# Three direct tiles instead of four, sixteen low halves of weights by adding transfers, and a written order of ScalarE and VectorE while x first arrives

## The chip, the cores and the metric

The kernel runs on one core of a Trainium2 chip. The time is that of the device in microseconds (us); before the change it is 864.02 us, the median of three runs (863.29 to 864.94). Lower is better. The engines are TensorE (PE, with its weight loads PEld), VectorE (DVE), ScalarE (ACT), GpSimd (POOL) and SyncE (SP); transfers are issued by SP, ACT or POOL and carried by 16 DMA engines.

## The reference

One decoder layer on x of 512 tokens by 1024 features, float32. A SwiGLU block, a mixing block and a second SwiGLU block each add to x:

```python
x = x + 0.5 * swiglu(rms_norm(x, g_ffn1[l]), w_ffn1_gate[l], w_ffn1_up[l], w_ffn1_down[l])
h = rms_norm(x, g_mix[l])
# attention, convolution and memory heads of h @ w_in
x = x + jnp.concatenate([y_attn, y_conv, y_mem], axis=-1) @ w_out[l]
x = x + 0.5 * swiglu(rms_norm(x, g_ffn2[l]), w_ffn2_gate[l], w_ffn2_up[l], w_ffn2_down[l])

def swiglu(x, w_gate, w_up, w_down):
    return (jax.nn.silu(x @ w_gate) * (x @ w_up)) @ w_down
```

The inner width of a SwiGLU block is 2816, which is 22 tiles of 128.

## The kernel before

x lies as eight tiles (k = 0 to 7) of 128 features by 512 tokens. A product of float32 operands is made of three matmuls: each operand is a high half (a copy rounded to the matmul's type) and a low half (the operand minus its high half), and `mm3` (L350 to L352) multiplies high by low, low by high and high by high. So each weight tile is split too. `Weights` does that for every load in a fixed list: SP's queue loads a raw tile of 128x1024, ScalarE copies the high half (L170), VectorE subtracts it from the raw tile (L171). Four raw buffers and four buffers of split weights turn by; a load is issued three items ahead of the split, and a split is written three items ahead of its use.

A SwiGLU block has 22 tiles f. The first `N_DIRECT` tiles are *direct*: 24 matmuls 128x512 for gate and 24 for up. Each later tile is *fast*: seven products of half width by a scheme like Strassen's (L447 to L449), 84 matmuls 128x256, on sums of weights (`make_sums`) and on sums of blocks of x (`blocks(k)`, k = 0 to 3, whose high and low halves are bh and bl). `evac` and `hidden` turn gate and up into the high and low half of a hidden tile (hh, hl). The product with the down weights comes in `ROUNDS`: as soon as the hidden tiles of a round exist, their part of all eight output tiles is computed and added to x, as items strewn between the fast tiles (`steps`), and the last round behind tile 21. Round 0 uses matmuls of full width, the others two halves. The first four results of round 0 are added to x by DMAs on POOL's queue (L506), others by VectorE (L509).

The norm's factor per token is found beside the first tile: squares of x on ScalarE (L372), sums on VectorE or POOL (L376), four small matmuls with `ones` (L381, `stats`), a chain on VectorE, then four transposes (L394) into `rb` (`spread`). The direct tiles run on x times the gain, and the factor `rb` comes in at `evac`. At the start x arrives in five loads (`STARTS`), and the weights of tile 0, w0 and w1, in two pieces each between them (`PIECES`), which `split_piece` splits (L182). At the end of the first block and of the mixing block, each finished tile of x is scaled and split (L361, L362) and its square added to the sum, for the norm of the next block. Items of the list have numbers: in the second SwiGLU block w130 and w131 are gate and up of tile 0, w132 and w133 of tile 1.

Apart from a few hand-written stretches a scheduler sets the order of each engine's instructions from the order of the code and the dependences; `tc.manual_schedule(engines=...)` keeps the written order for the engines named.

Of the kernel before, what the change touches and what calls it, by code (L numbers as in the profile page):

```python
# [38 lines left out]
P = 128  # L39
# [21 lines left out]
PIECES = {(0,): slice(0, 512), (2, 3): slice(512, 1024)}  # L61
# [15 lines left out]
ROUNDS = [(0, 4), (4, 8), (8, 12), (12, 16), (16, 18), (18, 22)]  # L77
N_DIRECT = 4
# [8 lines left out]
class Weights:  # L87
# [5 lines left out]
    def __init__(self, nc, pool, dma_ahead, conv_ahead, bufs):  # L93
        self.nc, self.pool = nc, pool
        self.dma_ahead, self.conv_ahead, self.bufs = dma_ahead, conv_ahead, bufs
        self.loads, self.items = [], []
        self.raw, self.after, self.split, self.piece = {}, {}, {}, {}
        self.sums = {}
        self.extra = None
        self.by_hand = 2  # L100
        self.loaded = self.done = self.at = self.turn = 0

    def add(self, ap, off=WIDE):
# [28 lines left out]

    def load_to(self, n):
        while self.loaded < min(n, len(self.loads)):
# [4 lines left out]
            if i >= self.by_hand:  # L139
                to = raw[:, : int(np.prod(ap.shape[1:]))]  # L140
                if len(ap.shape) == 3:
                    to = to.rearrange("p (a b) -> p a b", a=ap.shape[1])
                self.nc.sync.dma_start(to, ap)
            self.loaded += 1

    def split_to(self, n):
        nc = self.nc
        while self.done < min(n, len(self.items)):
# [17 lines left out]
            if i < self.by_hand:  # L166
                self.piece[i] = (src(), hi, lo)
            else:
                raw = src()
                nc.scalar.copy(hi[:, :cols], raw[:, :cols])  # L170
                nc.vector.tensor_tensor(lo[:, :cols], raw[:, :cols], hi[:, :cols].bitcast(F32), op=ALU.subtract)  # L171
# [5 lines left out]
    def load_piece(self, i, c):  # L177
        self.nc.sync.dma_start(self.piece[i][0][:, c], self.loads[i][:, c])
# [18 lines left out]
def steps(f):  # L197
# [4 lines left out]
    m = KT // per_load(0)  # L202
    if r == 1:
        i = f - ROUNDS[1][0]
        return [(0, g) for g in range(m - 1)] if i == 0 else [], [(0, m - 1)] if i == 1 else [], []

    queue = [(q, g) for q in range(1, len(ROUNDS) - 1) for g in range(KT // per_load(q))]
    return [], [queue[f - ROUNDS[2][0]]], []


def layer(tc, ctx, a):
# [35 lines left out]
    def ffn_weights(n, memory):  # L247
# [48 lines left out]

    nc.scalar.dma_start(par, a["par"])
    warm = tmp.tile([P, T], BF16, tag="t", name="warm", bufs=5)
# [7 lines left out]
    W.split_to(2)  # L306
    for ks in STARTS:
        nc.sync.dma_start(x[:, ks[0] : ks[-1] + 1], a["xT"][:, ks[0] : ks[-1] + 1])
        if ks in PIECES:
            for i in range(2):  # L310
                W.load_piece(i, PIECES[ks])
    W.load_to(4)
    nc.scalar.dma_start(ident, a["ident"])
# [50 lines left out]
    class Norm:  # L364
# [5 lines left out]
        def add(self, d, engine=POOL):  # L370
            sq = work() if d else tmp.tile([P, T], F32, tag="sqsum", name=nm("sqsum"), bufs=1)
            ACT.activation(sq, x[:, d], AF.Square)  # L372
            if d == 0:
                self.sum = sq
            else:
                (engine if d < KT - 1 else DVE).tensor_tensor(self.sum, self.sum, sq, op=ALU.add)  # L376

# [12 lines left out]
        def spread(self):  # L390
# [4 lines left out]
            DVE.tensor_copy(rb, ps)  # L395

    def ffn(pool, norm, first, gain, hooks, next_gain, last):
# [123 lines left out]
        for f in range(NF):  # L521
# [6 lines left out]
            else:  # L528
                g, u = (sc_bank(), sc_bank()) if f % 3 == 2 else (mm_bank(), mm_bank())
                gh, gl = W.next()  # L530
                if f == 0:
                    uh, ul = W.next()
                    for ks in first:
                        mm3(g, gh, gl, ks, xhk, xlk, ks[0] == 0, ks[-1] == 7)
                        mm3(u, uh, ul, ks, xhk, xlk, ks[0] == 0, ks[-1] == 7)
                    norm.stats()
                    held = (g, u)
                else:
# [29 lines left out]
    for ks in STARTS:  # L568
        for k in ks:
            scaled_split(k, C_G1)  # L570
        if ks in PIECES:
# [666 lines left out]
```

## Time and profile before

| | |
|---|---|
| median of three runs | 864.02 us |
| profiled execution | 864.32 us, of which 861.8 us are the span of the trace |
| matmuls of 128x256, fast tiles (L447 to L449) | 3 x 864, 716.0 us of printed durations |
| matmuls of 128x512, direct tiles (L350 to L352 with xh, xl) | 3 x 192, 226.7 us of printed durations |
| weights' high halves (L170), all forms | 122 and 72, 199.7 us on ACT |
| weights' low halves (L171), all forms | 122 and 72, 232.5 us on DVE |
| read from DRAM | 85.45 MB, 102 GB/s over the span |

A row of the trace's timeline gives start and duration in us, engine, line, operation and the tiles (out<-in) with their shape, then in brackets how long the engine was idle before it and what released it. A row of the waits gives who waited for whom, the us in total, how often, and the longest. Matmuls overlap, so the printed durations of TensorE add up to more than the time that they take.

### The profile page before, as it was taken

To read this page: it belongs to the slowest core of one execution; us is meant where nothing else is said; L and a number is where in the kernel's file an instruction comes from. 1 tells how busy PE (TensorE), PEld (TensorE's weight loads), DVE (VectorE), ACT (ScalarE), POOL (GpSimd) and SP (SyncE) were. 2 spreads that over 40 slices of the span, in tenths; PEclk is the share of its full clock that TensorE was granted. 3 is DMA by queue.
4 is the path that set the end of the run, shared out by engine and by line. 5 is a ranking of instruction groups with operands and counts; after the bars stand their busy time and mean duration, and the time that the engine had idled before them with its cause. 6 is when DMAs were issued, how large, how long until landed. Compare 5 with 4: busy or idle time off the path is not lost.

```text
span 861.8 us, 15658 instructions
## 1 busy us (share of the span) xinstructions
PE 854.5 (99%) x6361; PEld 790.9 (92%) x6361; DVE 696.6 (81%) x1163; ACT 445.9 (52%) x741; POOL 27.4 (3%) x30
## 2 busy tenths in 40 slices
PE   8999999999999999999999999999999999999998
PEld 5889999999999999988776888889999999999998
DVE  7998987777868797869988985998887868687772
ACT  7455555455644454533948763454654545545540
POOL 0010000000000000300000021010000000000000
PEclk9999999999999999999999999999999999999999
DMA  7335334243553334222010322335334343333312
GB/s 274 122 97 152 100 101 129 86 127 119 141 163 104 122 110 129 82 90 62 19 43 14 116 93 93 102 87 159 99 98 124 98 123 95 109 92 115 107 49 99
DMA packets 34808, 91.44 MB, mean 106 GB/s; under 512 B 3248, under 2 KB 5808, under 8 KB 34736
## 3 DMA queue, kind: packets, MB, share of 16 engines
q1 hardware_dynamic: 32000, 85.99, 32.0%
q0 software_dynamic: 1584, 2.88, 2.0%
q10 hardware_dynamic: 1152, 1.57, 0.6%
q8 instruction: 50, 0.82, 0.4%
q14 instruction: 22, 0.18, 0.1%
HBM read 85.45 MB, written 2.10 MB: 102 GB/s over the span
## 4 chain that ended last, share of the span: by engine, by line
PE 97%; DVE 1%; ACT 1%; DMA 1%; issue 0%; SPq 0%; ACTq 0%; DVEq 0%
PE mm L350 16%; PE mm L352 15%; PE mm L351 15%; PE mm L449 11%; PE mm L448 11%; PE mm L447 11%; PE sc L449 2%; PE sc L448 2%; PE sc L447 2%; PE tp L951 1%; PE sc L352 1%; PE sc L350 1%; PE sc L351 1%; PE sc L880 1%; PE tp L965 1%; PE mm L880 1%
## 5 line engine op out<-in xcount | busy, mean ns | idle before, releaser
L447 PE MATMUL mm<-bh,w 128*128 128x256 f32 x864 | 238.8, 276 | 0.0
L448 PE MATMUL mm<-bl,w 128*128 128x256 f32 x864 | 238.6, 276 | 0.0
L449 PE MATMUL mm<-bh,w 128*128 128x256 f32 x864 | 238.6, 276 | 0.0
L351 PE MATMUL mm<-hl,w 128*128 128x256 f32 (+1 forms) x640 | 183.7, 288 | 0.0
L352 PE MATMUL mm<-hh,w 128*128 128x256 f32 (+1 forms) x640 | 183.6, 287 | 0.0
L350 PE MATMUL mm<-hh,w 128*128 128x256 f32 (+1 forms) x640 | 183.1, 287 | 0.0
L170 ACT CAST w<-wraw 128x1024 fp32r<-128x1024 f32 (+2 forms) x122 | 124.0, 1020 | 86.1 <-PE mm L352 25.1
L171 DVE TENSOR_TENSOR w<-wraw,w 128x1024 fp32r<-128x1024 f32 (+2 forms) x122 | 144.5, 1189 | 28.4 <-ACT w L170 23.1
L447 PEld LDWEIGHTS mm<-bh,w 128*128 128x128 f32 x864 | 162.2, 188 | 0.2
L448 PEld LDWEIGHTS mm<-bl,w 128*128 128x128 f32 x864 | 162.2, 188 | 0.1
L449 PEld LDWEIGHTS mm<-bh,w 128*128 128x128 f32 x864 | 162.2, 188 | 0.0
L351 PEld LDWEIGHTS mm<-hl,w 128*128 128x128 f32 x640 | 120.1, 188 | 2.6 <-DVE hl L406 0.2
L352 PEld LDWEIGHTS mm<-hh,w 128*128 128x128 f32 x640 | 120.2, 188 | 2.5
L350 PEld LDWEIGHTS mm<-hh,w 128*128 128x128 f32 x640 | 120.1, 188 | 2.4
L171 DVE TENSOR_TENSOR w<-s,w 128x1024 fp32r<-128x1024 f32 x72 | 88.0, 1223 | 41.5 <-PE mm L449 34.6
L170 ACT CAST w<-s 128x1024 fp32r<-128x1024 f32 x72 | 75.7, 1051 | 24.8 <-PE mm L449 20.4
L350 PE MATMUL mm<-xh,w 128*128 128x512 f32 x192 | 75.8, 399 | 0.6 <-ACT w L182 0.6
L351 PE MATMUL mm<-xl,w 128*128 128x512 f32 x192 | 75.6, 394 | 0.6 <-DVE xl L362 0.5
L352 PE MATMUL mm<-xh,w 128*128 128x512 f32 x192 | 75.3, 392 | 0.0
L509 DVE SCALAR_TENSOR_TENSOR x<-mm,x 128x512 f32<-128x512 f32 x80 | 54.0, 683 | 1.8 <-PE mm L352 1.8
L468 ACT ACTIVATE t<-t 128x512 f32<-128x512 f32 x36 | 22.8, 633 | 61.7 <-DVE t L467 61.7
L127 DVE TENSOR_TENSOR s<-wraw 128x512 f32<-128x512 f32 x36 | 24.9, 691 | 28.8 <-DMA wraw<-in_wgu 28.6
(244 smaller groups left out, 1370.5 us busy)
## 6 DMA issues: line engine op xcount, KB each, us to landing
wraw<-in_wgu SPq DMA_DIRECT2D x86, 512.0 KB, 3.6
wraw<-in_wd SPq DMA_DIRECT2D x44, 512.0 KB, 3.6
wraw<-in_win SPq DMA_DIRECT2D x12, 512.0 KB, 3.5
x<-t POOLq DMA_DIRECT2D x8, 256.0 KB, 4.5
out<-t SPq DMA_DIRECT2D x7, 256.0 KB, 2.0
x<-in_xT SPq DMA_DIRECT2D x3, 512.0 KB, 6.3
wraw<-in_wout_a SPq DMA_DIRECT2D x6, 256.0 KB, 2.6
wraw<-in_wgu SPq DMA_DIRECT2D x4, 256.0 KB, 4.7
```

The source lines that it names most:

```text
L127: nc.vector.tensor_tensor(s12[:, l], u[:, l], u[:, r], op=ALU.add)
L170: nc.scalar.copy(hi[:, :cols], raw[:, :cols])
L171: nc.vector.tensor_tensor(lo[:, :cols], raw[:, :cols], hi[:, :cols].bitcast(F32), op=ALU.subtract)
L350: PE.matmul(ps[:, t], wh[:, w], hi(k)[:, t], start=one, stop=False, skip_group_check=cut > 1)
L351: PE.matmul(ps[:, t], wh[:, w], lo(k)[:, t], start=False, stop=False, skip_group_check=cut > 1)
L352: PE.matmul(ps[:, t], wl[:, w], hi(k)[:, t], start=False, stop=end, skip_group_check=cut > 1)
L447: PE.matmul(ps, wh[:, c], bh[k][:, block], start=one, stop=False, skip_group_check=not first)
L448: PE.matmul(ps, wh[:, c], bl[k][:, block], start=False, stop=False, skip_group_check=not first)
L449: PE.matmul(ps, wl[:, c], bh[k][:, block], start=False, stop=end, skip_group_check=not first)
L468: ACT.activation(g, g, AF.Silu)
L509: DVE.scalar_tensor_tensor(o, ps, 0.5, xd, op0=ALU.mult, op1=ALU.add)
L880: PE.matmul(banks[h][:, i * ML + c.start : i * ML + c.stop], self.q[rows, n * P : (n + 1) * P], self.kt[rows, ks], start=True, stop=True, ...
```

## The change

There are three parts.

1. `N_DIRECT` goes from 4 to 3, so tile 3 of each SwiGLU block becomes a fast tile, and the rounds become (0,3), (3,7), (7,11), (11,15), (15,19), (19,22). All four loads of round 0's down weights (128x768 each) are used ahead of tile 3. `hidden(f)` follows each direct tile, and the last direct tile also makes the blocks of k = 3.
2. Sixteen loads are marked `by_queue`: in each SwiGLU block the four of round 0, and gate and up of tile 2 in the first block and of tiles 0 to 2 in the second. For these ScalarE writes the negated high half into the low half's place, and a DMA on POOL's queue adds the weights onto it from DRAM.
3. At the start the pieces of w0 and w1 are columns 0 to 256, 256 to 512 and 512 to 1024, split behind k = 0, 2 and 4; the first ones come over ScalarE's queue, and `ident` comes on SP's queue. The order of ScalarE and SP while the loads are issued, and of ScalarE and VectorE in splits and squares, is the written one. In tile 0 the matmuls of gate and up alternate for the x tiles that arrive alone or in twos. `rb` is copied by ScalarE.

```diff
-PIECES = {(0,): slice(0, 512), (2, 3): slice(512, 1024)}
+PIECES = {0: slice(0, 256), 2: slice(256, 512), 4: slice(512, 1024)}
-ROUNDS = [(0, 4), (4, 8), (8, 12), (12, 16), (16, 18), (18, 22)]
-N_DIRECT = 4
+ROUNDS = [(0, 3), (3, 7), (7, 11), (11, 15), (15, 19), (19, 22)]
+N_DIRECT = 3
...
                 nc.scalar.copy(hi[:, :cols], raw[:, :cols])
-                nc.vector.tensor_tensor(lo[:, :cols], raw[:, :cols], hi[:, :cols].bitcast(F32), op=ALU.subtract)
+                if i in self.by_queue:
+                    nc.scalar.activation(lo[:, :cols], hi[:, :cols].bitcast(F32), AF.Copy, scale=-1.0)
+                    nc.gpsimd.dma_start(self.shaped(lo, self.loads[need]), self.loads[need], accum_op=ALU.add)
+                else:
+                    nc.vector.tensor_tensor(lo[:, :cols], raw[:, :cols], hi[:, :cols].bitcast(F32), op=ALU.subtract)
...
-    m = KT // per_load(0)
     if r == 1:
-        i = f - ROUNDS[1][0]
-        return [(0, g) for g in range(m - 1)] if i == 0 else [], [(0, m - 1)] if i == 1 else [], []
+        return [(0, g) for g in range(KT // per_load(0))] if f == N_DIRECT else [], [], []
...
-    return [], [queue[f - ROUNDS[2][0]]], []
+    i = f - ROUNDS[2][0]
+    return [], [queue[i]], queue[i + 1 :] if f == NF - 1 else []
...
-                W.add(down(*d), OTHER if d[0] else WIDE)
+                W.add(down(*d), OTHER if d[0] else WIDE, d[0] == 0)
             if f < N_DIRECT:
-                W.add(flat(gu[f, 0]))
-                W.add(flat(gu[f, 1]))
+                for i in range(2):
+                    W.add(flat(gu[f, i]), WIDE, n == 2 or f > 1)
...
+    W.split_to(2)
+    first = tc.manual_schedule(engines={mybir.EngineType.Activation, mybir.EngineType.SP})
+    first.__enter__()
     nc.scalar.dma_start(par, a["par"])
+    for i in range(2):
+        W.load_piece(i, PIECES[0], nc.scalar)
...
-    nc.scalar.dma_start(ident, a["ident"])
+    nc.sync.dma_start(ident, a["ident"])
+    first.__exit__(None, None, None)
...
-            DVE.tensor_copy(rb, ps)
+            ACT.copy(rb, ps)
...
+                        for k in ks:
+                            w = slice(k * P, (k + 1) * P)
+                            for i, (one, two) in enumerate(((0, xh), (0, xl), (1, xh))):
+                                for ps, both in ((g, (gh, gl)), (u, (uh, ul))):
+                                    PE.matmul(ps, both[one][:, w], two[k], start=k == i == 0, stop=k == 7 and i == 2)
...
-                    if f == 1:
-                        hidden(1, raw[1])
+                    hidden(f, raw[f])
                     blocks(f)
                 if f == N_DIRECT - 1:
-                    for i in range(2, N_DIRECT):
-                        hidden(i, raw[i])
+                    blocks(f + 1)
...
+    with tc.manual_schedule(engines={mybir.EngineType.Activation, mybir.EngineType.DVE}):
+        for k in range(KT):
             scaled_split(k, C_G1)
-        if ks in PIECES:
-            for i in range(2):
-                W.split_piece(i, PIECES[ks])
-    W.split_to(3)
-    for k in range(KT):
-        norm.add(k, DVE)
+            if k in PIECES:
+                for i in range(2):
+                    W.split_piece(i, PIECES[k])
+            if k in (3, 5):
+                sqs[k // 4] = norm.square(k // 4)
+            if k == 6:
+                take(0)
+                take(1)
+        W.split_to(3)
+        for k in range(2, KT):
+            sqs[k] = norm.square(k)
+            if k > 2:
+                take(k - 1)
+        take(KT - 1)
```

What the change moves is seen best in the instruction rows (line, operation, out<-in, shape). First ScalarE at the start of the program; xh is the high half of an x tile, a square's output is sqsum or t, and w0 and w1 are gate and up of tile 0. Before:

```order
L361 ACTIVATE xh_3_119<-x_69,par_67 128x512
L372 ACTIVATE sqsum_19_166<-x_69 128x512
L182 CAST w0_93<-wraw0_92 128x512
L182 CAST w1_95<-wraw1_94 128x512
L361 ACTIVATE xh_5_127<-x_69,par_67 128x512
L372 ACTIVATE t_20_168<-x_69 128x512
L361 ACTIVATE xh_7_131<-x_69,par_67 128x512
L372 ACTIVATE t_21_171<-x_69 128x512
L361 ACTIVATE xh_9_135<-x_69,par_67 128x512
L182 CAST w0_93<-wraw0_92 128x512
L182 CAST w1_95<-wraw1_94 128x512
```

and the same stretch now:

```order
L375 ACTIVATE xh_3_126<-x_69,par_67 128x512
L191 CAST w0_75<-wraw0_74 128x256
L191 CAST w1_77<-wraw1_76 128x256
L375 ACTIVATE xh_5_134<-x_69,par_67 128x512
L375 ACTIVATE xh_7_138<-x_69,par_67 128x512
L191 CAST w0_75<-wraw0_74 128x256
L191 CAST w1_77<-wraw1_76 128x256
L375 ACTIVATE xh_9_146<-x_69,par_67 128x512
L386 ACTIVATE sqsum_11_150<-x_69 128x512
L375 ACTIVATE xh_12_152<-x_69,par_67 128x512
L191 CAST w0_75<-wraw0_74 128x512
L191 CAST w1_77<-wraw1_76 128x512
```

The squares stand behind the casts now, and the second half of w0 and w1 is cast in two steps, its larger one behind x4.

Second, ScalarE where the second SwiGLU block begins. Before, w132 and w133 are gate and up of tile 1, w131 the up half of tile 0, xh_589 and xh_593 are x6 and x7:

```order
L170 CAST w132_5860<-wraw96_5731 128x1024
L372 ACTIVATE t_588_5852<-x_69 128x512
L361 ACTIVATE xh_589_5855<-x_69,par_67 128x512
L170 CAST w133_5903<-wraw97_5736 128x1024
L170 CAST w131_5822<-wraw95_5677 128x1024
L372 ACTIVATE t_592_5890<-x_69 128x512
L361 ACTIVATE xh_593_5893<-x_69,par_67 128x512
```

Now w136 and w137 are gate and up of tile 1, w135 the up half of tile 0, xh_592 and xh_596 are x6 and x7:

```order
L175 CAST w136_5970<-wraw98_5839 128x1024
L177 ACTIVATE w136_5970<-w136_5970 128x1024
L386 ACTIVATE t_591_5962<-x_69 128x512
L375 ACTIVATE xh_592_5965<-x_69,par_67 128x512
L175 CAST w137_6014<-wraw99_5845 128x1024
L177 ACTIVATE w137_6014<-w137_6014 128x1024
L175 CAST w135_5931<-wraw97_5785 128x1024
L386 ACTIVATE t_595_6001<-x_69 128x512
L177 ACTIVATE w135_5931<-w135_5931 128x1024
L375 ACTIVATE xh_596_6004<-x_69,par_67 128x512
```

Each cast has a negated copy (L177) behind it, and the square of x7 comes between the two of w135.

Third, POOL's queue and TensorE at the same place, after the change. On POOL, where only the sums stood before, the adding transfers stand among them:

```order
L393 TENSOR_TENSOR sqsum_572_5854<-sqsum_572_5854,t_587_5923 128x512
L178 DMA w136_5970<-in_wgu2 128x1024
L393 TENSOR_TENSOR sqsum_572_5854<-sqsum_572_5854,t_591_5962 128x512
L178 DMA w137_6014<-in_wgu2 128x1024
L178 DMA w135_5931<-in_wgu2 128x1024
L178 DMA w138_6020<-in_wgu2 128x1024
```

On TensorE, behind the first 21 matmuls of tile 0 (all with w134):

```order
L364 MATMUL mm_599_6013<-xh_573_5856,w135_5931 128x512
L365 MATMUL mm_599_6013<-xl_574_5857,w135_5931 128x512
L562 MATMUL mm_598_6012<-xh_596_6004,w134_5841 128x512
L562 MATMUL mm_598_6012<-xl_597_6005,w134_5841 128x512
L562 MATMUL mm_598_6012<-xh_596_6004,w134_5841 128x512
L401 MATMUL tp_600_6074<-ones_115,sqsum_572_5854 128x1 x4
L364 MATMUL mm_605_6096<-xh_573_5856,w136_5970 128x512
L365 MATMUL mm_605_6096<-xl_574_5857,w136_5970 128x512
L366 MATMUL mm_605_6096<-xh_573_5856,w136_5970 128x512
L364 MATMUL mm_605_6096<-xh_576_5870,w136_5970 128x512
L366 MATMUL mm_599_6013<-xh_573_5856,w135_5931 128x512
```

The last of these rows is the first matmul that reads w135's low half; the scheduler has put it behind the sums (L401) and four matmuls of tile 1's gate.

More of the change, by code (lines that the diff above doesn't have):

```diff
@@ L98, in __init__ @@
         self.sums = {}
+        self.by_queue = set()
         self.extra = None
@@ L101, in __init__, with add @@
         self.loaded = self.done = self.at = self.turn = 0
-    def add(self, ap, off=WIDE):
+    def add(self, ap, off=WIDE, by_queue=False):
+        if by_queue:
+            self.by_queue.add(len(self.items))
         self.loads.append(ap)
@@ L131, in make_sums, with shaped @@
         self.sums[i] = (s12, s43)
+    @staticmethod
+    def shaped(to, ap):
+        to = to[:, : int(np.prod(ap.shape[1:]))]
+        return to.rearrange("p (a b) -> p a b", a=ap.shape[1]) if len(ap.shape) == 3 else to
     def load_to(self, n):
@@ L175, in split_to, with load_piece @@
                 self.load_to(need + 1 + self.dma_ahead)
-    def load_piece(self, i, c):
-        self.nc.sync.dma_start(self.piece[i][0][:, c], self.loads[i][:, c])
+    def load_piece(self, i, c, queue):
+        queue.dma_start(self.piece[i][0][:, c], self.loads[i][:, c])
     def split_piece(self, i, c):
@@ L368, in __init__, with square, take @@
             self.sum = None
-        def add(self, d, engine=POOL):
+        def square(self, d):
             sq = work() if d else tmp.tile([P, T], F32, tag="sqsum", name=nm("sqsum"), bufs=1)
             ACT.activation(sq, x[:, d], AF.Square)
+            return sq
+        def take(self, d, sq, engine):
             if d == 0:
@@ L376, in add @@
                 (engine if d < KT - 1 else DVE).tensor_tensor(self.sum, self.sum, sq, op=ALU.add)
+        def add(self, d, engine=POOL):
+            self.take(d, self.square(d), engine)
         def stats(self):
@@ L533, in ffn @@
                     for ks in first:
-                        mm3(g, gh, gl, ks, xhk, xlk, ks[0] == 0, ks[-1] == 7)
-                        mm3(u, uh, ul, ks, xhk, xlk, ks[0] == 0, ks[-1] == 7)
+                        if len(ks) > 2:
+                            mm3(g, gh, gl, ks, xhk, xlk, ks[0] == 0, ks[-1] == 7)
+                            mm3(u, uh, ul, ks, xhk, xlk, ks[0] == 0, ks[-1] == 7)
+                            continue
+                        for k in ks:
[3 more added lines that the diff above has]
+                                    PE.matmul(ps, both[one][:, w], two[k], start=k == i == 0, stop=k == 7 and i == 2)
                     norm.stats()
@@ L567, in layer, with take @@
     norm = Norm()
-    for ks in STARTS:
-        for k in ks:
-            scaled_split(k, C_G1)
-        if ks in PIECES:
-            for i in range(2):
-                W.split_piece(i, PIECES[ks])
-    W.split_to(3)
-    for k in range(KT):
-        norm.add(k, DVE)
+    sqs = {}
+    def take(k):
+        norm.take(k, sqs.pop(k), DVE)
+    with tc.manual_schedule(engines={mybir.EngineType.Activation, mybir.EngineType.DVE}):
+        for k in range(KT):
+            scaled_split(k, C_G1)
+            if k in PIECES:
[12 more added lines that the diff above has]
+        take(KT - 1)
     mk = keep.tile([P, 2, ML], F32, name="mk")
```

10 lines of the change are left out of this document (4 added, 6 removed).

## The prediction

> **What bounds the kernel now.** I read the busy shares first, then the chain that ended last, then the waits of TensorE, and last the time from one matmul's start to the next.
>
> ```profile
> span 861.8 us, 15658 instructions
> PE 854.5 (99%) x6361; PEld 790.9 (92%) x6361; DVE 696.6 (81%) x1163; ACT 445.9 (52%) x741; POOL 27.4 (3%) x30
> PE 97%; DVE 1%; ACT 1%; DMA 1%; issue 0%; SPq 0%; ACTq 0%; DVEq 0%
> ...
> PE mm L350 <- DVE s L898: 1.0, 1, 1.0
> PE mm L350 <- ACT w L182: 0.6, 1, 0.6
> PE mm L351 <- DVE xl L362: 0.5, 1, 0.5
> ...
> 93.84 0.28 PE L447 MATMUL mm<-bh,w 128*128 128x256 f32 x1
> 112.89 0.28 PE L447 MATMUL mm<-bh,w 128*128 128x256 f32 x1
> ...
> 522.36 0.39 PE L350 MATMUL mm<-xh,w 128*128 128x512 f32 x1
> 533.24 0.95 PE L381 MATMUL tp<-ones,sqsum 128*128 128x1 f32 x8
> ```
>
> TensorE is busy for 99% of the span and holds 97% of the last chain; its longest waits are of 1 us. The kernel is a row of matmuls, so the time falls only if there are fewer of them, if they are smaller, or if one of the small waits goes, and it rises with every wait that a late operand adds. A matmul's printed duration overlaps the next one's, so I price one by the distance between starts. Two tiles of 84 matmuls 128x256 lie between 93.84 and 112.89: 19.05/168 = 0.1134 us each. One tile of 48 matmuls 128x512 lies between 522.36 and 533.24: 10.88/48 = 0.2267 us each. DVE, 81% busy, is the engine that can become a second bound, in some stages before others.
>
> **The sum, part by part.** It is made against the profiled execution: 861.8 us of span and 864.32 us in all. That execution is 0.30 us above the median of 864.02, so 0.30 is taken off at the end.
>
> *Tile 3 becomes a fast tile.* In each FFN 48 wide matmuls go (10.88 us) and 84 half-width ones come (84 x 0.1134 = 9.53 us). The down rounds cover the same 22 tiles, but round 0 now has three tiles: 24 fewer wide matmuls and 48 more half-width ones, which is 24 x 0.2267 = 5.44 against 5.44 us, nothing. Per FFN -1.35, for both **-2.70 us**. The program order bears the counts out: 144 wide matmuls fewer and 264 half-width more in all. What could take it back is the extra work of a fast tile on DVE, which is weighed under FFN1 below.
>
> *The start.*
>
> ```profile
> 6.10 0.50 PE L350 MATMUL mm<-xh,w 128*128 128x512 f32 x1 [0.60 <-ACT w L182]
> 12.48 0.74 PE L350 MATMUL mm<-xh,w 128*128 128x512 f32 x2
> 13.70 0.50 PE L351 MATMUL mm<-xl,w 128*128 128x512 f32 x1 [0.48 <-DVE xl L362]
> 19.74 0.95 PE L381 MATMUL tp<-ones,sqsum 128*128 128x1 f32 x8
> ...
> 8.40 0.72 ACT L361 ACTIVATE xh<-x,par 128x512 fp32r<-128x512 f32 x1
> 11.72 0.71 ACT L361 ACTIVATE xh<-x,par 128x512 fp32r<-128x512 f32 x1
> ...
> 2.12 0.91 SPq L308 DMA_DIRECT2D x<-in_xT  x2
> 4.66 0.43 SPq L308 DMA_DIRECT2D x<-in_xT  x1
> ...
> x<-in_xT SPq DMA_DIRECT2D x1, 512.0 KB, 5.8
> x<-in_xT SPq DMA_DIRECT2D x1, 512.0 KB, 6.3
> ```
>
> From 6.10 to 19.74 TensorE starts 52 wide matmuls, which need 52 x 0.2267 = 11.79 of these 13.64 us: 1.85 us are waits, and no order can win more than that behind the first matmul. The loads of x2,3 and x4,5 (the second issue of the row at 2.12 and the one at 4.66) land 5.8 and 6.3 us behind their issues at about 2.6 and 4.7, at 8.4 and 10.9; the cast of x2 begins at 8.40, when it lands. No order of ScalarE moves that wait. Behind x4,5 it can: ScalarE reaches that cast at 11.72, 0.8 us after the data, since it squares x and casts the second halves of w0 and w1 first, and TensorE waits between 12.48 and 13.70. Written out by hand with the casts first, my schedule has the 52 matmuls done at about 18.9: **-0.85 us**. Bounds: -1.9 when all waits go, +0.3 when the two small casts ahead of x2 delay it. The change also sends the first pieces of w0 and w1 over ScalarE's queue, half as long, and moves `ident` to the end of SP's queue; the transposes that read it come at 26 us, so that costs nothing.
>
> *The first normalization.* The evacuation of tile 0 waits for a chain on DVE.
>
> ```profile
> 20.72 0.16 DVE L383 TENSOR_SCALAR s<-tp 128x4 f32<-128x4 f32 x1 [0.41 <-PE tp L381]
> 20.80 1.23 DVE L171 TENSOR_TENSOR w<-wraw,w 128x1024 fp32r<-128x1024 f32 x1
> 22.08 1.22 DVE L171 TENSOR_TENSOR w<-wraw,w 128x1024 fp32r<-128x1024 f32 x1
> 24.98 0.43 DVE L386 COPY t<-rtok 128x512 f32<-128x512 f32 x1
> ```
>
> It takes 4.69 us, 2.45 of them two low halves; the ones of tile 2 now go by transfer, so 2.3 to 2.6 us are left. In the new order of TensorE 11 wide matmuls (2.5 us) stand between the sums and the transposes that need the chain. Wait 0 to 0.3: **+0.2 us**.
>
> *The sixteen transfers.* Each replaces a subtraction on DVE by a negated copy on ScalarE and a DMA that adds the weights from DRAM onto it. No operation like it is in the trace; the nearest are the adding transfers of 256 KB.
>
> ```profile
> L170 ACT CAST w<-wraw 128x1024 fp32r<-128x1024 f32 (+2 forms) x122 | 124.0, 1020 | 86.1 <-PE mm L352 25.1
> L171 DVE TENSOR_TENSOR w<-wraw,w 128x1024 fp32r<-128x1024 f32 (+2 forms) x122 | 144.5, 1189 | 28.4 <-ACT w L170 23.1
> ...
> L506 POOL DMA_DIRECT2D x<-t x8: 859/864/1211, 60.4 to 579.9; - x8
> DMA to landing us min/median/max: 3.4/4.5/7.8
> L611 POOL DMA_DIRECT2D mtot<-t x3: 859/859/862, 217.0 to 246.9; - x3
> DMA to landing us min/median/max: 3.3/5.2/5.3
> q0 software_dynamic: 576, 1.05, 41.7%
> ```
>
> DVE is relieved of up to 16 x 1.19 = 19 us, ScalarE takes on about 16 x 1.02 = 16 us at 52% busy, POOL 16 issues of 0.86 us; the 7.2 MB read a second time meet DMA engines that are busy for half of the time or less (0.50 and 0.35 in the windows quoted below). In place of 1.2 us the low half takes a copy and a landing. Four adding transfers hold 41.7% of 16 DMA engines in a stretch of 15 us, 1.56 us for each 256 KB, so for 512 KB I add 1.56 to the landing: 4.9 to 9.4 us, 6.1 by the median of L506, 6.8 by that of L611. In the order, fifteen of them are written early enough that this stays covered by a tile or more of matmuls. One is not.
>
> *The second FFN's first up weights.*
>
> ```profile
> 521.77 1.34 DVE L362 SCALAR_TENSOR_TENSOR xl<-x,par,xh 128x512 fp32r<-128x512 f32 x1 [1.38 <-ACT xh L361]
> 524.17 0.68 DVE L1132 TENSOR_TENSOR x<-mm,x 128x512 f32<-128x512 f32 x1
> 521.64 1.98 ACT L170 CAST w<-wraw 128x1024 fp32r<-128x1024 f32 x2
> ```
>
> The weight buffer of w135 (the up half of tile 0) comes free only when the last product of W_out ends, at 522.36. ScalarE then has, by the order, the end of w137's two copies (to about 523.0), w135's cast (to 524.0), the square of x7, which DVE delivers at about 523.8 since no low half stands ahead of its add any more, and w135's negated copy: the DMA is issued at about 525.45. Queued behind it on POOL are only w138's and later loads. TensorE needs that low half behind 26 matmuls of tile 0, the sums and four matmuls of tile 1: 522.36 + 30 x 0.2267 + 0.95 = 530.1. That is 4.65 us for a landing of 4.9 to 9.4: a wait of 0.2, 1.4 (L506's median), 2.1 (L611's) or 4.7 us. I take **+1.4 us**, by the median with the most samples.
>
> The Trainium skill ("DMA: Bandwidth & Descriptors", section "Anatomy of one DMA — SWDGE (gpsimd) path") fits a GpSimd-issued DMA by 2.0 us plus its bytes over 436e3 per us. By it 512 KB land in 3.2 us, an estimate, without a wait, and the sum would be rival B's. For 256 KB it gives 2.6 us; the trace has 3.3 to 7.8 for adding ones, so I give it less weight.
>
> *The end of FFN1, and the tiles between.*
>
> ```profile
> 361.20 1.34 DVE L362 SCALAR_TENSOR_TENSOR xl<-x,par,xh 128x512 fp32r<-128x512 f32 x1 [1.38 <-ACT xh L361]
> 360.69 1.30 POOL L376 TENSOR_TENSOR sqsum<-sqsum,t 128x512 f32<-128x512 f32 x1 [2.02 <-ACT t L372]
> ...
> 42.00:69.20 27.20, 27.20 (x121) 22.37 (x120) 26.99 (x39) 14.65 (x19) 3.62 (x4) 1.00 0.50 126
> 69.20:113.00 43.80, 43.80 (x363) 42.78 (x362) 37.09 (x49) 24.54 (x38) 0.00 (x0) 1.00 0.35 110
> ```
>
> The last round holds three tiles instead of four: one output step of it is 18 half-width matmuls (2.04 us) instead of 24 (2.72). DVE has per step the add to x (0.68), the low half of x (1.34 beside POOL's sum) and now and then a low half of weights, so its lead shrinks by about 0.7 us a step and reaches zero at the last ones: 0 to 0.5, **+0.1 us**. In the windows (columns: length, then TensorE, its weight loads, DVE, ScalarE, POOL) DVE is busy 26.99 of 27.20 us from 42 to 69, in the stretch of tile 3 and round 0, and 37.09 of 43.80 behind it. There six low halves leave DVE in the first FFN (tile 2's two and round 0's four, which have 768 columns now) and ten in the second, against one more tile of block sums and of hidden values; by hand every operand comes 0.4 us or more ahead. I take nothing; bounds 0 and +2.
>
> **Sum**: -2.70 - 0.85 + 0.2 + 1.4 + 0.1 = -1.85; 864.32 - 1.85 - 0.30 = **862.2 us**.
>
> **Rivals.** *B: w135's transfer lands in time.* For it speaks the shortest landing, 3.4 us, with little else in flight; against it that w137's load is issued 2.5 us ahead of it and w138's soon behind. Without the 1.4 us: 860.8.
> *C: the landing grows with the bytes in full, and the result is slower.* Twice 5.2 is 10.4 us; 10.4 - 4.65 = 5.75 us of wait in place of 1.4: 866.5. It decides against the change from a landing of about 9.6 us on. For it speaks the 7.8 us that a 256 KB transfer once took, against it that most took near 4.5. In the Trainium skill ("SBUF — State Buffer", the box on DVE blocking a DMA) a GpSimd-issued DMA cannot write its descriptors while DVE holds their common port; by that rule a long DVE operation at 525 us brings C. The 0.86 us of the issues, beside a DVE 99% busy at 60 us, show no such lock but for the one of 1.21.
> *D: the start gains nothing,* because x arrives as late as before and the smaller casts fill what the squares left: 862.2 + 0.85 = 863.0. For it: the cast of x2 at 8.40 stands at the landing itself, and nothing in the change makes x come sooner.
> *E: DVE is late in round 0 or at FFN1's end* by 1.3 us more than summed: 863.5. For it the 26.99 of 27.20; against it the low halves taken off.
>
> **How the numbers follow.** The forecast has 0.43, B 0.18, C 0.15, D 0.13, E 0.11. A measurement here tells about 0.2%, 1.7 us, from no change: faster is below 862.3, slower above 865.7. Faster: all of B, 0.26 of the forecast's (its bounds lie on both sides of 862.3) and 0.01 of D, 0.45. Slower: C, 0.15. Within: the rest, 0.40. The range goes from 860.0 (B with some more of the start's waits gone) to 865.5 (E with 2 us more, or half of C) and leaves out about 2 in 10.
>
> **What would show it.** A wait of TensorE for the low half of w135 (a DMA, at the second FFN's first tiles) of 0.7 to 2.1 us; none is B, over 5 is C. The sums of squares at 18.6 to 19.2 us instead of 19.74; at 19.6 it is D. 144 and 264 matmuls at 0.2267 and 0.1134 us. Any wait of TensorE for `hh`, `hl`, block sums or `xl` of over 0.5 us between 40 and 75 or at 355 to 365 is E. A wait for another of the sixteen transfers would prove my covers wrong.

## The result, and the profile after

The changed kernel takes 868.15 us (median of eight runs, 867.22 to 873.35) against 863.85 for the kernel before in the same comparison (863.14 to 864.94). The ratio is 1.006, with a 95% interval of 1.0039 to 1.008: it is slower, and above the upper end of the predicted range, 865.5.

The page of the changed kernel, the same lines as before the change, and below them its waits of TensorE (who waited for whom, us in total, times, longest):

```profile
span 866.6 us, 15985 instructions
PE 852.9 (98%) x6481; PEld 793.5 (92%) x6481; DVE 688.7 (79%) x1162; ACT 468.0 (54%) x778; POOL 46.0 (5%) x46
PE 85%; DVE 6%; ACT 3%; DMA 3%; issue 2%; ACTq 0%; POOL 0%; DVEq 0%; POOLq 0%
...
PE mm L366 <- DMA w<-in_wgu: 3.2, 1, 3.2
PE mm L364 <- ACT hh L425: 1.4, 1, 1.4
...
PE mm L467 <- ACT kept L482: 0.8, 1, 0.8
...
PE mm L365 <- DVE xl L376: 0.7, 1, 0.7
PE mm L467 <- DVE x L529: 0.4, 1, 0.4
```

TensorE's printed busy time fell by 1.6 us and the span grew by 4.8. The chain that ended last shows it: TensorE holds 85% of it now and not 97%, and VectorE, ScalarE and the DMAs, which held 1% each, hold 12% together. Two of the waits are longer than any before, and the three below them are new or longer too. Where the time comes from is seen by the start of the same matmul in both traces, first of the mixing block and first of the second FFN; the second's counterpart before is the row at 522.36.

```profile
358.06 0.40 PE L350 MATMUL mm<-xh,w 128*128 128x512 f32 x1
```

```profile
358.69 0.40 PE L364 MATMUL mm<-xh,w 128*128 128x512 f32 x1
...
522.22 0.39 PE L364 MATMUL mm<-xh,w 128*128 128x512 f32 x1
```

By my terms the first FFN should have ended 2.0 us earlier (1.35 + 0.85 - 0.2); it ends 0.6 us later, so 2.6 us were lost in it. The mixing block makes up 0.8, which is no merit of the change (last section). From 522.22 to the end 344.4 us pass, against 339.4: the second FFN alone is 4.9 us longer, though it has 1.35 us less to multiply.

The largest wait, in the timeline of the changed kernel (start, duration, engine, line, operation): the DMA of w135's low half on POOL, then TensorE's last matmul ahead of that low half, the first that reads it, and two of those behind.

```profile
525.92 0.86 POOL L178 DMA_DIRECT2D w<-in_wgu  x1 [1.54 <-ACT w L177]
...
529.72 0.40 PE L364 MATMUL mm<-xh,w 128*128 128x512 f32 x1
533.33 0.50 PE L366 MATMUL mm<-xh,w 128*128 128x512 f32 x1 [3.21 <-DMA w<-in_wgu]
533.66 0.58 PE L364 MATMUL mm<-xh,w 128*128 128x512 f32 x1
534.04 0.63 PE L365 MATMUL mm<-xl,w 128*128 128x512 f32 x1
```

The view of that one transfer (size, us from issue to landing) and of the stretches around it (length, TensorE, its weight loads, VectorE, ScalarE, POOL, the clock granted to TensorE, the share of the DMA engines, GB/s):

```profile
w<-in_wgu POOLq DMA_DIRECT2D x1, 512.0 KB, 7.4
...
526.00:530.00 4.00, 4.00 (x23) 3.18 (x21) 1.55 (x7) 1.89 (x3) 0.78 (x1) 1.00 1.01 222
530.00:533.30 3.30, 0.11 (x1) 0.00 (x0) 1.46 (x8) 0.45 (x1) 1.04 (x1) 1.00 1.06 254
533.30:537.00 3.70, 3.67 (x9) 2.90 (x10) 0.00 (x0) 0.00 (x0) 0.00 (x0) 0.55 0.79 138
```

It is issued at 525.92 and lands 7.4 us later, at 533.3; TensorE needs it at 529.95 and stands 3.4 us. Behind the wait its matmuls start 0.43 us apart, not 0.227: the granted clock is 0.55 for 3.7 us, and nine matmuls cost 1.7 us more. Together 5.1 us. The DMA engines are busy throughout (1.01 and 1.06). From the issue to the landing it is these two queues that fill them, POOL's with the adding transfers (q0) and SP's with raw loads (q1); the columns are packets, MB and the share of the 16 engines' time:

```profile
q0 software_dynamic: 269, 0.97, 71.9%
q1 hardware_dynamic: 522, 0.76, 30.3%
```

POOL spends its usual 0.86 us on the issue, and between it and 529 us VectorE runs one operation, of 0.75 us; so nothing here shows a long VectorE operation holding the transfer up, which the prediction's rival C thought possible.

In the first FFN, from the same trace: ScalarE, VectorE and TensorE around hidden tile 2, the last one that round 0 needs.

```profile
38.11 0.62 ACT L175 CAST vhi<-wraw 128x512 fp32r<-128x512 f32 x1 [2.15 <-DMA wraw<-in_wgu]
41.49 0.63 ACT L434 ACTIVATE t<-t 128x512 f32<-128x512 f32 x1
...
44.30 0.68 DVE L436 TENSOR_TENSOR kept<-sc,rb 128x512 f32<-128x512 f32 x1
44.90 0.74 DVE L446 SCALAR_TENSOR_TENSOR braw<-x,par,rb 128x512 f32<-128x512 f32 x1
45.56 1.22 DVE L460 TENSOR_TENSOR bl<-bmade,bh 128x1024 fp32r<-128x1024 f32 x1
46.69 0.68 DVE L437 TENSOR_TENSOR kept<-kept,t 128x512 f32<-128x512 f32 x1
...
48.08 1.20 PE L364 MATMUL mm<-hh,w 128*128 128x512 f32 x4 [1.35 <-ACT hh L425]
```

The product that becomes hidden tile 2 (L437) waits behind two operations on blocks, 1.8 us, and ScalarE stood still 2.15 us for a raw load earlier, with the activation that L437 needs (L434) queued behind. That raw load, issued at 32.28, took 5.8 us to land. TensorE waits 1.4 us for hh.

Two theories came out of this. *Theory 1*: the transfers cost the time, w135's directly, the others by holding up raw loads and ScalarE. *Theory 2*: three direct tiles leave VectorE too little time ahead of round 0, and the transfers are only what hides part of it.

### The profile page after: what moved, and what is told of

Read it like the earlier page. It is cut to its first block, busy times and chain, and to the rows that moved or that the text cites. A ratio compares the mean times of both kernels' runs of the same rounds, so it can differ in the third digit from the quotient of the medians.

```text
span 866.6 us, 15985 instructions
## 1 busy us (share of the span) xinstructions
PE 852.9 (98%) x6481; PEld 793.5 (92%) x6481; DVE 688.7 (79%) x1162; ACT 468.0 (54%) x778; POOL 46.0 (5%) x46
## 4 chain that ended last, share of the span: by engine, by line
PE 85%; DVE 6%; ACT 3%; DMA 3%; issue 2%; ACTq 0%; POOL 0%; DVEq 0%; POOLq 0%
PE mm L364 13%; PE mm L366 12%; PE mm L365 12%; PE mm L467 11%; PE mm L469 11%; PE mm L468 11%; PE sc L469 2%; PE sc L468 2%; PE sc L467 2%; DMA wraw<-in_wgu 2%; DVE w L180 2%; PE mm L562 1%; PE tp L989 1%; ACT p L954 1%; DMA w<-in_wgu 1%
## 5 line engine op out<-in xcount | busy, mean ns | idle before, releaser
L467 PE MATMUL mm<-bh,w 128*128 128x256 f32 x912 | 252.3, 277 | 1.2 <-ACT kept L482 0.8
L468 PE MATMUL mm<-bl,w 128*128 128x256 f32 x912 | 251.9, 276 | 0.0
L469 PE MATMUL mm<-bh,w 128*128 128x256 f32 x912 | 251.9, 276 | 0.0
L364 PE MATMUL mm<-hh,w 128*128 128x256 f32 (+1 forms) x656 | 185.8, 285 | 1.4 <-ACT hh L425 1.4
L366 PE MATMUL mm<-hh,w 128*128 128x256 f32 (+1 forms) x656 | 186.3, 284 | 0.0
L467 PEld LDWEIGHTS mm<-bh,w 128*128 128x128 f32 x912 | 171.2, 188 | 1.7 <-ACT kept L482 1.0
L468 PEld LDWEIGHTS mm<-bl,w 128*128 128x128 f32 x912 | 171.2, 188 | 0.0
L469 PEld LDWEIGHTS mm<-bh,w 128*128 128x128 f32 x912 | 171.2, 188 | 0.0
L180 DVE TENSOR_TENSOR w<-wraw,w 128x1024 fp32r<-128x1024 f32 (+2 forms) x108 | 125.4, 1162 | 40.4 <-ACT w L175 38.4
L364 PEld LDWEIGHTS mm<-hh,w 128*128 128x128 f32 x656 | 123.0, 188 | 3.8 <-ACT hh L425 2.0
L366 PEld LDWEIGHTS mm<-hh,w 128*128 128x128 f32 x656 | 123.1, 188 | 1.8
L366 PE MATMUL mm<-xh,w 128*128 128x512 f32 x142 | 56.4, 397 | 3.2 <-DMA w<-in_wgu 3.2
L364 PE MATMUL mm<-xh,w 128*128 128x512 f32 x142 | 57.5, 405 | 0.0
L365 PE MATMUL mm<-xl,w 128*128 128x512 f32 x142 | 56.7, 399 | 0.7 <-DVE xl L376 0.7
L175 ACT CAST vhi<-wraw 128x512 fp32r<-128x512 f32 x38 | 23.6, 621 | 48.0 <-PE sc L468 41.7
```

Source lines behind the costliest of these rows:

```text
L364: PE.matmul(ps[:, t], wh[:, w], hi(k)[:, t], start=one, stop=False, skip_group_check=cut > 1)
L365: PE.matmul(ps[:, t], wh[:, w], lo(k)[:, t], start=False, stop=False, skip_group_check=cut > 1)
L366: PE.matmul(ps[:, t], wl[:, w], hi(k)[:, t], start=False, stop=end, skip_group_check=cut > 1)
L467: PE.matmul(ps, wh[:, c], bh[k][:, block], start=one, stop=False, skip_group_check=not first)
L468: PE.matmul(ps, wh[:, c], bl[k][:, block], start=False, stop=False, skip_group_check=not first)
L469: PE.matmul(ps, wl[:, c], bh[k][:, block], start=False, stop=end, skip_group_check=not first)
```

## The experiments

Each was timed in five rounds against the kernel before, on one chip for each group (e1 to e4, e5 to e8, e9 to e11, e12); rows of different groups are best compared by their ratios. Waits and stretches are those of one profiled run of each kernel. Lines of after are meant unless said otherwise.

| kernel | what | us | ratio to before, interval |
|---|---|---|---|
| as changed | all three parts | 868.15 | 1.006 [1.0039, 1.008] |
| e1 | no transfers | 870.62 | 1.0081 [1.0065, 1.0097] |
| e2 | w135 by VectorE | 863.23 | 0.9994 [0.9984, 1.0004] |
| e3 | w137 by VectorE | 868.13 | 1.0044 [1.0027, 1.0061] |
| e4 | first FFN without transfers | 874.32 | 1.0109 [1.0089, 1.0129] |
| e5 | start alone | 864.15 | 1.0004 [0.9995, 1.0012] |
| e6 | three direct tiles alone | 870.53 | 1.0082 [1.0068, 1.0097] |
| e7 | four direct tiles, start and transfers, w135's counterpart by VectorE | 863.06 | 0.9992 [0.9983, 1.0001] |
| e8 | e2, last rounds of three and four | 863.27 | 0.9994 [0.9985, 1.0003] |
| e9 | e2, first FFN's tile 2 by VectorE | 864.36 | 1.0006 [0.9997, 1.0016] |
| e10 | e2, one more transfer in tile 1 | 864.32 | 1.0003 [0.9993, 1.0012] |
| e11 | e2, blocks of k = 3 later | 872.19 | 1.0099 [1.0084, 1.0114] |
| e12 | as changed, w135's low half used last | 866.59 | 1.0027 [1.0014, 1.0039] |

**e1, no transfers.**

```diff
-        if by_queue:
+        if False:
             self.by_queue.add(len(self.items))
```

> All sixteen low halves come from VectorE again; tiles, rounds and the start stay as changed. Theory 1 (the adding transfers cost the time: the low half of w135 lands 7.4 us behind its issue, TensorE waits 3.4 us and then runs 3.5 us at half clock; in the first FFN the same transfers hold up raw loads, ScalarE and the hidden tile 2, 1.4 + 0.6 us): 868.15 - 5.1 - 2.0 = about 861, no wait for w135 and none over 0.5 us between 40 and 65 us. Theory 2 (three direct tiles leave too little work ahead of round 0, whatever makes the low halves; only w135 is the transfers' fault): 863, with the wait for hh near 47 us as it is or longer. Theory 3 (VectorE is too full without the transfers): over 864, waits of TensorE for low halves by VectorE.

870.62, over both ends that blame the transfers. The time is theory 3's; its sign is met only in part, for TensorE waits for x and hh, and for a low half (hl) just 0.3 us. Below are the stretch from 34 to 62 us in the kernel before, in the changed one, and in e1, and e1's two longest waits.

```profile
34.00:62.00 28.00, 28.00 (x125) 23.02 (x124) 27.79 (x41) 15.54 (x20) 1.62 (x2) 1.00 0.24 76
```

```profile
34.00:62.00 28.00, 26.20 (x121) 21.35 (x120) 26.24 (x40) 17.88 (x25) 7.10 (x7) 1.00 0.76 158
```

```profile
34.00:62.00 28.00, 24.59 (x107) 19.55 (x105) 28.00 (x43) 16.03 (x22) 3.65 (x4) 1.00 0.39 95
...
PE mm L467 <- DVE x L529: 5.0, 2, 2.9
PE mm L364 <- ACT hh L425: 2.1, 1, 2.1
```

VectorE was busy for 27.79 of 28 us already, beside a TensorE that never stood. In e1 it is busy all 28 and TensorE loses 3.4 of them. Removing 10.9 us of direct matmuls ahead of round 0 took the time in which VectorE worked off that list, and the wait for `hh` is its sign. So the transfers are on the useful side of the account in the first FFN, and theory 1 falls there as a forecast of the time. What it says of raw loads is seen all the same: the two that are issued at 25.65 and 32.28 us in the changed kernel land after 9.3 and 5.8 us, their counterparts in e1 after 4.4 and 3.4.

**e2, w135 by VectorE.**

```diff
-W.add(flat(gu[f, i]), WIDE, n == 2 or f > 1)
+W.add(flat(gu[f, i]), WIDE, (n == 2 or f > 1) and (n, f, i) != (2, 0, 1))
```

> Of the sixteen, only the low half of w135 (up of tile 0, second FFN) goes back to VectorE. If the wait for it costs 3.4 us and the half clock behind it 1.7: 868.15 - 5.1 = 863.0, TensorE at full clock from 530 to 540 us. If the half clock has nothing to do with the wait, it stays and the time is 864.7. If the next transfer in the row (w137 or w138) is late then as well, a new wait of 1 to 3 us shows up within 5 us and the time is 864 to 866.

863.23: one of sixteen transfers costs 4.9 us by the medians (5.7 by the ratios), as the trace said. TensorE at the same place, at full clock:

```profile
530.00:533.30 3.30, 3.30 (x16) 2.73 (x15) 0.00 (x0) 0.00 (x0) 0.00 (x0) 1.00 0.02 5
```

Without it the change is worth nothing that can be told from no change. By the sum it should be worth 3 us; e5 to e9 ask where those are.

**e3, w137 by VectorE** (the condition excludes (2, 1, 1) instead).

> Only the low half of w137, whose transfer runs just ahead of w135's, goes back to VectorE; w135 keeps its transfer. Theory queue (two adding transfers of one queue share it, and w135's waits for w137's): w135 lands 5.6 to 5.9 us behind its issue, as w134 and w136 did, TensorE waits about 2 us instead of 3.4, and the time is 865 to 866.5. Theory size (a transfer of 512 KB takes 7 us by itself): it lands 7.4 us behind its issue and the time stays within 0.5 us of 868.

The transfer of w135 and the wait in e3:

```profile
w<-in_wgu POOLq DMA_DIRECT2D x1, 512.0 KB, 6.7
...
530.42 0.50 PE L366 MATMUL mm<-xh,w 128*128 128x512 f32 x1 [3.37 <-DMA w<-in_wgu]
```

It lands after 6.7 us with its neighbour gone: between the two theories. The time says nothing on either, since the scheduler also drew the first reader of the low half forward by the sums and four matmuls, so that the wait stayed 3.4 us. From 524 to 531 us the adding transfers hold 43.2% of the DMA engines' time and the raw loads 44.7%, against 71.9 and 30.3% in the changed kernel. Engines that are nearly full, with the neighbour's bytes as much as with raw loads, remain the likeliest cause of the 7.4; it is not shown.

**e4, the first FFN without transfers.**

```diff
-W.add(down(*d), OTHER if d[0] else WIDE, d[0] == 0)
+W.add(down(*d), OTHER if d[0] else WIDE, n == 2 and d[0] == 0)
...
-W.add(flat(gu[f, i]), WIDE, n == 2 or f > 1)
+W.add(flat(gu[f, i]), WIDE, n == 2)
```

> The six transfers of the first FFN go back to VectorE, the ten of the second stay. Theory 1 (the transfers there delay raw loads, and with them ScalarE and hidden tile 2): the wait for hh near 47 us and the one near 61 us go, -2.0 us by then; the time 866 to 866.5. Theory 2 (too little work between tile 2 and round 0): the wait for hh stays within 0.3 us of 1.4 or grows with VectorE's load, and the time is 868 to 869. If the mixing block takes up what is won ahead of it, the gain shows at 400 us and is gone at 500.

874.32, 6.2 us over the changed kernel by the medians and 4.2 by the ratios: more than theory 2 said, and against theory 1. The wait for `hh` rises to 2.1 us and one of 1.8 for x comes; in the profiled run 3.4 us at half clock follow each of them, which costs about 1.7 us more each. The six transfers of the first FFN are worth four to six microseconds, part of them half clock.

**e5, the start alone**, with four direct tiles, the old rounds and no transfers.

> Four direct tiles, the old rounds and all low halves by VectorE; only the new start, the new order of its splits and squares, and rb by ScalarE. If the start is worth what the trace of the changed kernel shows (the first 52 matmuls begin within 13.3 us of the first instead of 13.6, and 0.3 us sooner; 0.3 us lost before the transposes): 863.3 to 863.5 beside 863.7 to 863.9. If the start's gain only shifts a wait into the next stage: the same as before within 0.1 us, with a new wait between 20 and 70 us.

864.15, the same as before within the interval. The first 52 matmuls are done earlier, but a wait of 0.6 us for `hl` comes near 58 us, on the VectorE that is full in that stretch: the second case.

**e6, three direct tiles alone**, on the start of before and with no transfers (lines of before, shifted by one).

> Three direct tiles and the new rounds alone, on the start of before and with all low halves by VectorE. If VectorE cannot feed round 0 and the first fast tile of the first FFN without the transfers: 870 to 872, waits for hh of about 2 us near 47 and for the add of round 0 (x) of 2 to 3 us near 60 us, as without the transfers. If it is the new start that makes VectorE late there: 863 to 865 without these waits.

870.53, the first case by its time and by the waits for x; a wait for `hh` does not come. The stretch and the two largest sums of waits (those for xl lie at the start and at the end of the first FFN):

```profile
34.00:62.00 28.00, 25.25 (x113) 20.59 (x112) 28.00 (x42) 16.16 (x21) 3.65 (x4) 1.00 0.43 98
...
PE mm L446 <- DVE x L508: 5.1, 2, 2.8
PE mm L350 <- DVE xl L361: 1.2, 2, 0.8
```

Tile 3's change to a fast tile, with its new rounds, by itself costs 6.9 us, for all that it takes 2.7 us of matmuls away: VectorE is busy 28.00 of 28 us, and the first fast tile of each FFN waits for it (2.8 and 2.4 us, for x).

**e7, four direct tiles with start and transfers** (three of round 0's four loads and tiles 2, or 0 to 2, as in the change; w135's counterpart by VectorE).

> Four direct tiles and the old rounds, the new start, and the adding transfers for the same loads but w135's counterpart (13 of them, since one of the old round 0's loads stands elsewhere). If the transfers are worth something only where VectorE is the bound, which it is not with four direct tiles: within 0.3 us of the start alone. If they harm by delaying raw loads and filling ScalarE: 864 to 866, with waits for hh or low halves near 35 to 60 and 530 to 560 us. If they help by themselves: under 862.5.

863.06, at the edge of an effect: 1.1 us under e5, with no wait of TensorE over 0.1 us between 34 and 62 us:

```profile
34.00:62.00 28.00, 28.00 (x125) 23.09 (x125) 27.88 (x43) 18.55 (x25) 5.39 (x5) 1.00 0.66 146
```

The transfers that come in time seem to pay a little with the old tiles as well, as e5's wait is gone, but the intervals of the two overlap; none of the three cases met it exactly.

**e8, the last rounds** on e2.

```diff
-(11, 15), (15, 19), (19, 22)]
+(11, 15), (15, 18), (18, 22)]
```

> The kernel with w135 by VectorE, and the last two rounds cut as (15, 18) and (18, 22), so that a step of the last round has 24 half-width matmuls as before, not 18. If the short steps make xl6 late at the end of the first FFN (0.9 us of waits near 362 us in the changed kernel, 0.3 before): that wait goes and the time is 0.6 less than with w135 alone on VectorE, 862.6. If the mixing block takes up what is won ahead of it, or a round of three tiles is as bad one place earlier: 863.2, the same.

```profile
PE mm L365 <- DVE xl L376: 0.8, 1, 0.8
```

The wait for xl6 is as long with steps of 24 matmuls, and the time the same. My reason for it, the short steps, falls; what lengthened it is open.

**e9, tile 2 of the first FFN by VectorE** on e2 (the condition is `n == 2 and (f, i) != (0, 1)`).

> On the kernel with w135 by VectorE, the two low halves of tile 2 in the first FFN go back to VectorE too; the four of its round 0 keep their transfers. If these two transfers, which land 7 and 10 us behind their issues while raw loads wait, are what makes ScalarE stand still for the raw load of tile 3 (2.2 us at 36 us in the changed kernel) and hidden tile 2 late: the wait for hh near 46 us goes, 862.0 to 862.5. If VectorE is the bound there, its 2.4 us more come back as waits between 25 and 62 us: 864.5 to 866.

The wait for `hh` goes to under 0.3 us, but it was 0.3 in e3 too, which has all six transfers there, so one profile doesn't show that the edit did it. Waits of 0.7 us for `vhi` and for x come near 60 us; the time is by ratio 1.2 thousandths above e2, with intervals that overlap. Neither the raw load nor VectorE alone decides there; relief at one place is paid at the next.

**e10, one more transfer**, tile 1's up of the first FFN (`or (f, i) == (1, 1)` in the condition), on e2.

> On the kernel with w135 by VectorE, the low half of tile 1's up weights in the first FFN also goes by an adding transfer. If VectorE is the bound from the first normalization to round 0: its 1.2 us less bring the factor rb and all behind it forward, the waits near 26, 46 and 60 us (0.4 + 0.8 + 0.6) shrink by about 1 us in all, 862.2 to 862.6. If the transfers' queue is the bound: those of tile 2 land later still, waits for them or for hh over 1 us, 864 or more.

```profile
PE mm L366 <- DMA w<-in_wgu: 1.7, 1, 1.7
```

The second case's mechanism at a smaller price: TensorE waits 1.7 us at 28 us for the new transfer (and in the profiled run has 3.4 us at half clock behind it), while the waits between 40 and 62 us vanish, where TensorE comes later now; 864.32, against 864.32 for the kernel before on that chip.

**e11, blocks of k = 3 behind round 0** on e2.

```diff
                 if f == N_DIRECT - 1:
-                    blocks(f + 1)
...
+            if f == N_DIRECT:
+                blocks(f)
             if f >= N_DIRECT:
                 fast(f, mid)
```

> On the kernel with w135 by VectorE, the blocks of k = 3 are written behind round 0, not behind tile 2, in both FFNs. If they stand in hidden tile 2's way on VectorE: the waits for hh near 46 and 560 us (0.8 + 0.4) go and nothing else comes, 862.0 to 862.4. If VectorE has too much to do in that stretch whatever its order: the first fast tile waits for bh or bl of k = 3, or for block sums, by 1 us or more in each FFN, 863.5 to 866.

Here these blocks are formed from x after round 0 has begun to be added to it, so what comes out is not the layer any more, and the run tells only of times. 872.19: the first fast tile waits for `bh` 4.2 us in two places and for the low half `vlo` 1.0. Putting off this work of VectorE and ScalarE costs more than it gives.

**e12, the low half of w135 last**, with all sixteen transfers.

```diff
+                    if last:
+                        with tc.manual_schedule(engines={mybir.EngineType.PE}):
+                            mm3(g, gh, gl, range(8), xhk, xlk, True, True)
+                            norm.stats()
+                            for two in (xh, xl):
+                                for k in range(8):
+                                    PE.matmul(u, uh[:, k * P : (k + 1) * P], two[k], start=k == 0 and two is xh, stop=False)
+                            for k in range(8):
+                                PE.matmul(u, ul[:, k * P : (k + 1) * P], xh[k], start=False, stop=k == 7)
```

> All sixteen transfers stay, w135's too. In tile 0 of the second FFN TensorE keeps a written order: all of gate, the sums, then the 16 products of up with w135's high half, then the 8 with its low half, so that 40 matmuls stand ahead of the first reader of the low half and not 30. If the place of that reader and the landing, 7.4 us behind the issue, are the whole of it: the need moves from 529.95 to 532.2 us, the wait from 3.4 to about 1.1, and, if the half clock comes from the long wait, that goes too: 868.15 - 2.3 - 1.7 = 864.2. If the half clock has another cause: 865.8, with the granted clock near 0.5 for 3 us behind 533 us. If the transfer is held up by something that moves with TensorE: the wait stays over 3 us and the time at 868.

```profile
529.05 0.86 POOL L178 DMA_DIRECT2D w<-in_wgu  x1 [1.54 <-ACT w L177]
...
w<-in_wgu POOLq DMA_DIRECT2D x1, 512.0 KB, 8.0
...
537.14 1.20 PE L561 MATMUL mm<-xh,w 128*128 128x512 f32 x4 [1.60 <-DMA w<-in_wgu]
```

866.59: the wait is 1.6 us, with a landing 0.6 us later than reckoned, and no half clock behind it. The time is above both cases all the same; in the profiled run (868.13) the wait for `hh` in the first FFN, where nothing was changed, is 1.9 us, with 3.4 us at half clock behind it. By ratios 2.9 us of the change's loss of 5.2 are recovered (0.0033 of 864). The place of the first reader against the landing sets the length of this wait; part of the loss can be had back by order, nearly all of it by VectorE (e2).

## Why the prediction was wrong

*The count of matmuls* was right: 144 wide ones less and 264 half-width more run at their old distances, and no experiment shows otherwise.

*The start* was sized right and booked wrong. In the changed kernel the first matmul and the one behind the 52nd are these; before they stand at 6.10 and 19.74:

```profile
5.76 0.50 PE L562 MATMUL mm<-xh,w 128*128 128x512 f32 x1 [0.34 <-ACT w L191]
...
19.00 0.39 PE L365 MATMUL mm<-xl,w 128*128 128x512 f32 x1
```

That is 0.75 us earlier (0.85 predicted). Between 20 and 40 us 0.45 us of it are lost again, in gaps between matmuls around the first normalization (0.2 predicted). But e5 has no gain in time: what is won ahead of a stretch in which VectorE is full comes back there as a wait. Rival D's price was right, for another reason than the arrival of x.

*The tiles between* are the first step that failed: "by hand every operand comes 0.4 us or more ahead. I take nothing; bounds 0 and +2". Measured: around round 0 of the first FFN the gaps between matmuls grew by 2.4 us with the transfers, 1.4 of it the wait for `hh` and 0.4 that for x; without them tile 3's change cost 6.9 us net of the saving (e6). The row that said so was quoted: 26.99 of 27.20 us busy. I read it as near the limit. What e1 and e6 show is that VectorE had no room at all there: of the 10.9 us of direct matmuls that each FFN loses ahead of round 0, e6 gets about 3.8 us back as gaps between 40 and 120 us, and in the second FFN 5.2 us behind 545 us. The work of VectorE per FFN had to be set against TensorE's new length of the stretch, not margins at single operands.

With the transfers VectorE is no longer full there (26.24 of 28 us), and another cause sets the wait for `hh`. In five kernels ScalarE, VectorE and TensorE have the same order in that stretch: the changed one, e2, e3, e8 and e12. The raw load that ScalarE stands for lands 5.8, 5.1, 4.7, 5.4 and 6.3 us behind its issue, and the wait is 1.4, 0.6, 0.3, 0.9 and 1.9 us: it moves with the landing, nearly one for one. The load and the wait in e3, the least, and in e12, the most:

```profile
wraw<-in_wgu SPq DMA_DIRECT2D x1, 512.0 KB, 4.7
...
PE mm L364 <- ACT hh L425: 0.3, 1, 0.3
```

```profile
wraw<-in_wgu SPq DMA_DIRECT2D x1, 512.0 KB, 6.3
...
PE mm L364 <- ACT hh L425: 1.9, 1, 1.9
```

That a raw load lands late beside the transfers had no term either. The 0.8 us for `kept` is a third thing, in a fast tile of the second FFN at 622 us; its cause is open.

*w135* is the second, and the larger one here. The mechanism was right, even its times: issue at 525.9 (525.45 predicted), need at 530.0 (530.1). Two sizes were off. The landing took 7.4 us, not 6.1. The price of a transfer was a good median and a bad bet; all sixteen in one row:

```profile
DMA to landing us min/median/max: 5.1/6.2/11.0
```

The ones that run beside others are the long ones, 10.5 and 11.0 us for two issued near 25 us and 6.8 to 7.4 for three issued between 523 and 531, and w135's was one of those by its place: w137's runs just ahead, raw loads beside. The prediction set the transfers against DMA engines busy for half of the time or less, by windows of the first FFN; at w135's place they were full (1.01 and 1.06). (The bytes read twice are 7.34 MB by the two pages of the profile, not 7.2; nothing hangs on it.) The Trainium skill's fit ("DMA: Bandwidth & Descriptors", "Anatomy of one DMA — SWDGE (gpsimd) path") gives an estimate of 3.2 us for 512 KB. The shortest of the sixteen took 5.1 us, for 384 KB, so the landing that rival B needed, under 4.65 us, never came. And the 1.7 us at half clock behind the wait were in no term.

*The end of FFN1* had 0.1 and took 0.6, by a cause that e8 did not confirm.

The sum of the measured terms, in us, each the gaps between matmuls beyond their usual distance in that stretch (the tiles: the count of matmuls), after minus before: -2.7 tiles, -0.75 start, +0.45 first normalization, +2.4 in round 0 of the first FFN, +0.6 at its end, +5.1 w135, +1.2 in the rest of the second FFN, -1.3 in the mixing block; together +5.0, against 4.8 in the spans. Rival C named the right place and sign at a chance of 0.15; its price, from a landing of 10.4 us, was not what came true. E's sign came true beside it, a wait for `hh` of over 0.5 us between 40 and 75 us, though the late raw load set its length. I had treated the two as alternatives, and they add up.

## What to carry to other kernels

Where a second engine is busy for the whole of a stretch, the length of that stretch is set by both: cutting the first one's work ahead of it bought nothing here but waits. A transfer that replaces an operation of 1.2 us wins where its landing has several microseconds of cover in the program order, and loses all at the one place where it has less; find the first reader of each, and price the landing by the crowded cases of the trace. e2 with three direct tiles and e7 with four end within 0.2 us of each other: what the smaller number of matmuls saved was lost again in TensorE's waits.

## What the runs showed of the hardware

TensorE ran at half its clock in stretches of 3.4 us. One follows the wait of 3.4 us (0.55 over 3.7 us, above). The Trainium skill ("TensorE: Matmul & The Clock Gate", "Part 1: The HAM clock gate (the "warmup" mystery)") has the clock halved behind an idle window of about 3.4 us that runs free of the program. The trace agrees in the length of the stretch, and not in the idle time ahead of it: in the profiled runs half clock also followed waits of 1.7 us (e10), 1.8 and 2.1 (e4), 1.9 (e12) and 2.9 (e1). It did not follow those of 2.8 and 2.4 us in e6. That the window runs free would fit this, and e3, where a wait as long had full clock behind it in the profiled run, here with the wait ahead:

```profile
526.60:530.40 3.80, 0.45 (x2) 0.02 (x1) 0.00 (x0) 2.10 (x2) 0.86 (x1) 1.00 0.78 170
530.40:534.00 3.60, 3.58 (x16) 2.95 (x17) 0.00 (x0) 0.00 (x0) 0.00 (x0) 1.00 0.95 165
```

The profiled run of e3 took 866.39 us, 1.7 less than its median, which is about the price of one such stretch. But the kernel before has such a stretch too, in the mixing block, with no wait ahead of it that is longer than a microsecond, and the changed one has none there:

```profile
455.00:459.00 4.00, 4.00 (x20) 2.81 (x19) 3.26 (x26) 3.13 (x10) 0.00 (x0) 0.57 0.28 72
```

```profile
455.00:459.00 4.00, 3.78 (x29) 2.78 (x28) 3.70 (x28) 4.00 (x15) 0.00 (x0) 1.00 0.28 68
```

That is the 1.3 us by which the mixing block looks shorter after the change: in the fourteen profiled runs, from its first matmul to the second FFN's, it takes 164.3 to 164.8 us in the seven that have a half-clock stretch in it, and 162.8 to 163.6 in the seven that have none. It is one reason why single profiles of this kernel can differ by 1 to 2 us where nothing was done.
